# Expert steps of 512 columns a block, four places for split weights, and a written-out order of three engines, in a two-layer decoder trunk

## The chip, the cores and the metric

The kernel runs on one core of one Trainium2 chip. The metric is device time of the whole program in microseconds (us); one program computes both layers of the trunk. The engines are named PE (TensorE, matmuls), DVE (VectorE), ACT (ScalarE), POOL (GpSimd) and SP (SyncE, which only issues the loads of weights). Each engine works through its own queue in order.

## The reference

A residual stream `x` of 256 tokens by 1024 channels goes through two layers. Each layer has four token mixers and an output projection, a layer norm, a feed-forward part, a gated embedding `ple`, and a second layer norm. The feed-forward part of the second layer is a mixture of eight experts, of which each token uses two:

```python
D_MODEL, SEQ, D_FF_EXPERT, N_EXPERTS, TOP_K, MOE_BLOCK = 1024, 256, 3584, 8, 2, 128

def moe_swiglu(x, w_router, w_gate, w_up, w_down):
    logits = (xf @ w_router).astype(jnp.float32)
    top_val, top_idx = lax.top_k(logits, TOP_K)
    top_w = jax.nn.softmax(top_val, axis=-1)
    ...                      # the rows of each expert are brought together, 128 to a block
    def expert_block(args):
        xe, e = args
        return (jax.nn.silu(xe @ w_gate[e]) * (xe @ w_up[e])) @ w_down[e]
    ...                      # each row times its weight, added back to its token

        x = layer_norm(ALPHA * x + mixed, ln1_g[i], ln1_b[i])
        f = moe_swiglu(x, moe_router[i // 2], moe_w_gate[i // 2], moe_w_up[i // 2], moe_w_down[i // 2])
        ple = jax.nn.sigmoid(x @ ple_w_gate[i]) * (p[i] @ ple_w_proj[i])
        x = layer_norm(ALPHA * x + f + ple, ln2_g[i], ln2_b[i])
```

All data are float32. The weights of one expert are three matrices of 1024 x 3584 numbers, 44 MB.

## The kernel before

**Split products.** To keep float32 accuracy on PE, each weight block is split into a high piece (`whi`, made by ACT in L191) and a low piece (`wlo`, raw minus high, made by DVE in L193), and each product is three matmuls (`mm3`, L248 to L250): high by high, high by low (L249, the only one that reads `wlo`), low by high.

**Stream of weights.** `Stream` holds a list of blocks. SP loads a block into a raw buffer as soon as one is free (L157); eleven raw buffers take part in the expert stage. `take` hands out the pieces of a block, and before that calls `ahead`, which writes the splits of as many blocks as there are places for split pieces: three, the block in use among them. A place is free again when PE has done the block that stood there.

**Expert stage.** The gathered 128 rows of an expert (`rows`, by an indirect DMA of POOL from `x_rows`) are transposed by PE (`gat`) and split (`gh`/`gl`, `ghl`). Then follow four steps `j` of 896 hidden columns. `up` runs two products (`fg`, `fu`) into four banks `pff` of 448 columns each, in eight blocks (896 KB each, 12 matmuls each); ACT applies Silu to `fg` (L1512) and DVE multiplies by `fu` (L1513, tile `ffg`). `turn` transposes the 896 columns (`ftp`, L1522) and splits them (`hth`, `htl`, L565 and L566). `down` takes the `w_down` blocks of the step before (three or four, 1 MB, 12 matmuls of 512 columns each) and sums into two banks `pdn` for the whole expert. The order on PE is so: up of step j, then down of step j-1. An expert has 32 up-blocks and 14 down-blocks. PSUM banks come from two groups of four: `mm_bank` (`pff`, `ppg`) and `ax_bank` (`pdn`, `ftp`, `gat` and others).

**Side work.** Generators (`start_side`) hold work that is dealt out between blocks: `pump()`, called after every block, counts each down and runs it to its next `yield`. So `prepare` gathers the rows of the next expert, `collect` adds up the results at the end, and `turn` is one too.

**Hand-over.** Before the experts, DVE normalises two tiles of 128 tokens (L603, L604), PE transposes them (`xtp`), the router's product (`lp`) and the top-2 choice follow on PE, ACT and DVE (`lg`, `sel`, `gw`, `pos`), and four quarters of the gate product of the embedding (`ppg`, 48 matmuls of 256 columns each) run on PE meanwhile; their results are finished by DVE (`plt`) and POOL.

**Order.** In this part the program's order on SP is fixed by hand (`manual_schedule`); the order of PE, DVE, ACT and POOL is the scheduler's choice.

Of the kernel before, what the change touches and what calls it, by code (L numbers as in the profile page):

```python
# [20 lines left out]
P = 128  # L21
T = 256
NT = 2
# [74 lines left out]
def tile_trunk(ctx, tc, x, p, positions, w_in, s5_a_re, s5_a_im, s5_log_dt, s5_b_re, s5_b_im, s5_c_re, s5_c_im,  # L98
# [33 lines left out]
    class Stream:  # L132
# [41 lines left out]
        def double(self, slots):  # L174

            self.pair = [(q[0], m) for q, m in zip(self.pair, slots)]
# [940 lines left out]
    FE, PAIRS = 896, ((0, 3), (3, 7), (7, 10), (10, 14))  # L1117

    def plan_experts(add, units, wg, wu, wd, r_in, r_out, per=2):

        last = None
        of = lambda r: (r,) if per == 1 else ()

        def down():
            e, j = last
            for c in range(*PAIRS[j]):
                for r in range(0, 2, per):
                    add(("fd", e, c) + of(r), r_out(wd, e, 2 * c + r, per), [(ALL, ALL)])

        for e in units:  # L1130
            for j in range(4):
                for nm, w in (("fg", wg), ("fu", wu)):
                    for q in range(4):
                        for r in range(0, 2, per):
                            add((nm, e, j, q) + of(r), r_in(w, e, 2 * q + r, per, FE * j, FE), [(ALL, ALL)])
                if last:
                    down()
                last = e, j
        down()
# [5 lines left out]
    def down_rows(t, r0, c, n):  # L1145

        first = lambda c: r0 + FE * (c // 7) + c % 7
        return dr(t, first(c) * D, [[7 * D, P], [(first(c + 1) - first(c)) * D, n], [1, D]])
# [334 lines left out]
    def experts(units, before, down_end):  # L1483


        def pair(u, *key):

            if u.get("per") == 1:
                return [[t[:, 0] for t in u["take"](*key, r)] for r in range(2)]
            w = u["take"](*key)  # L1490
            return [[t[:, r] for t in w] for r in range(2)]

        def up(u, j):
            bk = {}
            hi, lo = u["x"]
            cols_ = [slice(FE // 2 * h, FE // 2 * (h + 1)) for h in range(2)]
            for w in ("fg", "fu"):
                bk[w] = [mm_bank("pff")[:, 0:FE // 2] for _ in range(2)]
                for q in range(4):
# [27 lines left out]
        def down(u, j, side_):  # L1527
# [3 lines left out]
            for c in range(*PAIRS[j]):  # L1531
                ab = pair(u, "fd", c)
# [418 lines left out]
```

## Time and profile before

| | |
|---|---|
| median of three runs | 1881.46 us (1880.41 to 1882.23) |
| profiled execution | 1881.37 us, span 1879.6 us |
| mean granted clock of PE in it | 0.986 of full speed |
| PE busy | 1807.0 us (96%) |
| DVE, ACT, POOL busy | 1451.9 us (77%), 1136.7 us (60%), 290.7 us (15%) |
| moved by DMA | 506.16 MB, mean 269 GB/s |
| expert stage | 860.16 to 1858.95 us of the span |

The shares are means over the whole program, in which the mixers of both layers, the dense feed-forward part of the first layer and the experts have different limits. The expert stage is more than half of the time; after it stand some 20 us for the last combination, layer norm and the store.

### The profile page before, as it was taken

The page shows a single profiled execution, that of the slowest core. Times are in us where ns is not written, and L with a number is a line of the kernel's source. Part 1 is how long each engine was busy: PE and PEld are TensorE (multiplying, and loading weights), DVE is VectorE, ACT ScalarE, POOL GpSimd, SP SyncE. Part 2 cuts the span into 40 slices and gives each one's busy share as a digit, 9 for nine tenths or more (in the row PEclk, how much of TensorE's full clock was granted, in tenths as well). Part 3 has the DMA queues.
Part 4 walks back from the last instruction along what each step waited for, and adds up shares of the span by engine and source line. Part 5 has one row for each costly group of instructions (what it writes and reads, how often), then busy time and mean ns, then how long its engine had stood idle before and what let it go on. Part 6 is the DMA issues. An engine that isn't in the chain of part 4 may idle for free. (4 is left out here: it accounts for less than half of the span.)

```text
span 1879.6 us, 26683 instructions
## 1 busy us (share of the span) xinstructions
PE 1807.0 (96%) x10669; PEld 1627.9 (87%) x10669; DVE 1451.9 (77%) x1392; ACT 1136.7 (60%) x1143; POOL 290.7 (15%) x286
## 2 busy tenths in 40 slices
PE   8999999999999999997999999999999999999995
PEld 7889989999978989986888888888888888888884
DVE  7966687554476865777888888888888988888886
ACT  5544454444435454455777777677777777777772
POOL 2755238000031210231100000000000000000011
PEclk9999999999999999998999999999999999999998
DMA  7443466555534338846999999899999999999981
GB/s 247 144 123 113 163 235 202 188 192 181 183 131 138 136 110 316 277 166 227 379 349 383 371 361 375 324 368 381 357 366 335 368 366 366 359 381 356 366 341 47
DMA packets 166681, 506.16 MB, mean 269 GB/s; under 512 B 15852, under 2 KB 30740, under 8 KB 154260
## 3 DMA queue, kind: packets, MB, share of 16 engines
q1 hardware_dynamic: 163460, 493.36, 71.7%
q0 software_dynamic: 2080, 7.35, 1.0%
q10 hardware_dynamic: 1008, 3.67, 0.5%
q8 instruction: 85, 1.39, 0.3%
q14 instruction: 48, 0.39, 0.1%
HBM read 497.52 MB, written 6.82 MB: 268 GB/s over the span
## 5 line engine op out<-in xcount | busy, mean ns | idle before, releaser
L193 DVE TENSOR_TENSOR wlo<-raw,whi 128x1792 fp32r<-128x1792 f32 (+1 forms) x368 | 769.8, 2104 | 122.1 <-ACT whi L191 92.3
L191 ACT ACTIVATE whi<-raw 128x1792 fp32r<-128x1792 f32 (+1 forms) x368 | 649.6, 1770 | 229.2 <-PE pff L250 118.6
L193 DVE TENSOR_TENSOR wparts<-raw,wparts 128x1024 fp32r<-128x1024 f32 (+1 forms) x235 | 306.0, 1308 | 188.8 <-ACT wparts L191 187.8
L191 ACT ACTIVATE wparts<-raw 128x1024 fp32r<-128x1024 f32 (+1 forms) x244 | 254.9, 1050 | 256.8 <-PE pff L250 79.3
L249 PE MATMUL pff<-wlo,ghl 128*128 128x448 f32 x896 | 328.0, 366 | 3.4 <-DVE wlo L193 3.3
L250 PE MATMUL pff<-whi,ghl 128*128 128x448 f32 x896 | 328.1, 366 | 0.0
L248 PE MATMUL pff<-whi,ghl 128*128 128x448 f32 x896 | 292.3, 369 | 0.8 <-ACT whi L191 0.8
L249 PE MATMUL pdn<-wlo,hth 128*128 128x512 f32 x448 | 179.0, 399 | 11.5 <-DVE wlo L193 11.3
L249 PEld LDWEIGHTS pff<-wlo,ghl 128*128 128x128 f32 x896 | 168.4, 188 | 20.8 <-DVE wlo L193 4.9
L250 PEld LDWEIGHTS pff<-whi,ghl 128*128 128x128 f32 x896 | 168.8, 188 | 15.5
L248 PEld LDWEIGHTS pff<-whi,ghl 128*128 128x128 f32 x896 | 166.6, 188 | 15.1 <-ACT whi L191 1.3
L250 PE MATMUL pdn<-whi,htl 128*128 128x512 f32 x448 | 178.4, 398 | 0.0
L248 PE MATMUL pdn<-whi,hth 128*128 128x512 f32 x448 | 159.9, 397 | 0.5 <-ACT whi L191 0.5
L250 PE MATMUL pgt<-xh,wparts 128*128 128x256 f32 x512 | 146.8, 287 | 1.7 <-DVE wparts L193 1.7
L249 PE MATMUL pgt<-xl,wparts 128*128 128x256 f32 x512 | 146.7, 287 | 0.0
L248 PE MATMUL pgt<-xh,wparts 128*128 128x256 f32 x512 | 146.6, 287 | 0.0
L249 PE MATMUL pff<-xl,wparts 128*128 128x256 f32 x448 | 126.5, 282 | 0.0
L248 PE MATMUL pff<-xh,wparts 128*128 128x256 f32 x448 | 126.4, 282 | 0.0
L250 PE MATMUL pff<-xh,wparts 128*128 128x256 f32 x448 | 126.4, 282 | 0.0
L249 PEld LDWEIGHTS pdn<-wlo,hth 128*128 128x128 f32 x448 | 84.9, 190 | 33.2 <-DVE wlo L193 15.3
L250 PEld LDWEIGHTS pgt<-xh,wparts 128*128 128x128 f32 x512 | 98.9, 193 | 2.6 <-DVE wparts L193 1.9
L250 PEld LDWEIGHTS pdn<-whi,htl 128*128 128x128 f32 x448 | 85.1, 190 | 18.2
(570 smaller groups left out, 3161.3 us busy)
## 6 DMA issues: line engine op xcount, KB each, us to landing
raw<-in_moe_w_gate_dram SPq DMA_DIRECT2D x128, 896.0 KB, 6.9
raw<-in_moe_w_up_dram SPq DMA_DIRECT2D x128, 896.0 KB, 7.5
raw<-in_moe_w_down_dram SPq DMA_DIRECT2D x112, 1024.0 KB, 7.2
raw<-in_w_in_dram SPq DMA_DIRECT2D x49, 1024.0 KB, 5.1
raw<-in_ff_w_gate_dram SPq DMA_DIRECT2D x14, 1024.0 KB, 5.0
raw<-in_ff_w_up_dram SPq DMA_DIRECT2D x14, 1024.0 KB, 5.0
raw<-in_ff_w_down_dram SPq DMA_DIRECT2D x14, 1024.0 KB, 4.9
raw<-in_w_branch_dram SPq DMA_DIRECT2D x8, 1024.0 KB, 5.0
```

The costliest lines, as they stand in the source:

```text
L191: S.activation(hi, src, AF.Copy)
L193: eng.tensor_tensor(lo, src, hi.bitcast(F32), op=OP.subtract)
L248: PE.matmul(o, ah, bh, start=start, stop=False)
L249: PE.matmul(o, ah, bl, start=False, stop=False)
L250: PE.matmul(o, al, bh, start=False, stop=stop)
```

## The change

- The steps of an expert are 1024, 1024, 1024 and 512 columns (`STEPS`), in up to two banks of 512 columns for each of the two products. A block of `w_gate` or `w_up` is 1 MB: 256 rows x 1024 columns, or 512 rows x 512 columns in the last step. An expert has 28 up-blocks and 14 down-blocks of 12 matmuls of 512 columns each.
- A partition gets four rows of `w_down` of a 512-row group instead of seven of an 896-row group.
- There are four places for split pieces; raw buffers go from eleven to nine.
- PE, DVE and ACT follow the order of the program from the first step of the routing to the end of the experts.
- Work is dealt out in smaller parts: `turn` does one multiply, one group of four transposes, or one split at a time; Silu comes after the first `fu` block; `gat` comes in two groups of four, each split one block later; the scaled store of an expert's result (`store`) and the last combination (`final`) are dealt out too. `prep` of the next expert starts one step earlier and waits six blocks for its rows.

```diff
         def double(self, slots):
-            self.pair = [(q[0], m) for q, m in zip(self.pair, slots)]
+            self.pair = [(q[0], m) for q, m in zip(self.pair + [(slots[0], None)], slots)]
...
-    FE, PAIRS = 896, ((0, 3), (3, 7), (7, 10), (10, 14))
+    STEPS = (2, 2, 2, 1)
...
         def up(u, j):
...
+            n = STEPS[j]
+            k = 4 // n
+
+            g = [ph["pool"].tile([P, 4, P], F32, tag="ffg", bufs=3, name="ffg") for _ in range(n)]
+            turned = lambda b: b.rearrange("t (p c) -> t c p", c=4)
             for w in ("fg", "fu"):
-                bk[w] = [mm_bank("pff")[:, 0:FE // 2] for _ in range(2)]
-                for q in range(4):
-                    ab = pair(u, w, j, q)
-                    for h in range(2):
-                        for r in range(2):
-                            kk = 2 * q + r
-                            mm3(bk[w][h], hi[:, kk, :], lo[:, kk, :], *(t[:, cols_[h]] for t in ab[r]),
+                bk[w] = [mm_bank("pff") for _ in range(n)]
+                for q in range(KD // k):
+                    ab = block(u, k, w, j, q)
+                    for h in range(n):
+                        for r in range(k):
+                            kk = k * q + r
+                            mm3(bk[w][h], hi[:, kk, :], lo[:, kk, :], *(t[:, 512 * h:512 * h + 512] for t in ab[r]),
                                 kk == 0, kk == KD - 1)
+                    if (w, q) == ("fu", 0):
+                        for h in range(n):
+                            S.activation(g[h], turned(bk["fg"][h]), AF.Silu)
                     pump()
-            g = tmp("ffg", [P, FE])
-            for h in range(2):
-                gs = g.rearrange("t (c p) -> t c p", c=7)[:, :, P // 2 * h:P // 2 * (h + 1)]
-                fg, fu = (bk[w][h].rearrange("t (p c) -> t c p", c=7) for w in ("fg", "fu"))
-                S.activation(gs, fg, AF.Silu)
-                V.tensor_tensor(gs, gs, fu, op=OP.mult)
             def turn():
-                yield 1
-                h2 = [ph["pool"].tile([P, 7, P], F32R, tag="ht" + t, bufs=2, name="ht" + t) for t in "hl"]
-                u.setdefault("h", {})[j] = h2
-                for a, n in ((0, 4), (4, 3)):
+                for h in range(n):
+                    V.tensor_tensor(g[h], g[h], turned(bk["fu"][h]), op=OP.mult)
+                    yield 1
+                for h in range(n):
                     tp = ax_bank("ftp")
-                    for c in range(n):
-                        PE.transpose(tp[:, c * P:(c + 1) * P], g[:, (a + c) * P:(a + c + 1) * P], ident)
-                    split_out(*(t[:, a:a + n, :].rearrange("p c t -> p (c t)") for t in h2), tp[:, 0:n * P])
+                    for c in range(4):
+                        PE.transpose(tp[:, c * P:(c + 1) * P], g[h][:, c, :], ident)
+                    yield 1
+                    h2 = [ph["pool"].tile([P, 4, P], F32R, tag="ht" + t, bufs=2, name="ht" + t) for t in "hl"]
+                    u.setdefault("h", {})[2 * j + h] = h2
+                    split_out(*(t.rearrange("p c t -> p (c t)") for t in h2), tp)
...
-            yield 3 if e.get("first") else 5
+            yield 3 if e.get("first") else 6
...
                     PE.transpose(b[:, k * P:(k + 1) * P], xg[:, ks], ident)
+                yield 1
                 split_out(*(t[:, 4 * k4:4 * k4 + 4, :].rearrange("p k t -> p (k t)") for t in (gh, gl)), b)
                 yield 1
...
         state = {"p": start_side(first_rows())}
+        order = tc.manual_schedule(engines={mybir.EngineType.PE, mybir.EngineType.DVE, mybir.EngineType.Activation})
+        order.__enter__()
         step_side(state["p"])
...
-        ws.double([more] * HL_BUFS)
+        ws.double([more] * (HL_BUFS + 1))
...
-            if j == 2 and e + 1 < NE:
+            if j == 1 and e + 1 < NE:
                 state["p"] = start_side(prep(e + 1))
...
         experts(es, before, down_end)
+        order.__exit__(None, None, None)
```

The order on the engines moves at three places. The first is PE's queue at the hand-over: `pp` and `ohp` are small products of the routing, `gat` the transposes of the gathered rows, `pff` the first expert product. Before:

```order
L249 MATMUL ppg<-wparts,xh 128x256
L250 MATMUL ppg<-wparts,xl 128x256
L1636 MATMUL pp<-sel,cst 128x16
L1637 MATMUL pp<-sel,ones 128x16
L1658 MATMUL ohp<-wt,oh 128x2 x2
L1682 MATMUL gat<-cst,rows 128x128 x8
L248 MATMUL pff<-whi,gh 128x448
L249 MATMUL pff<-wlo,gh 128x448
L248 MATMUL pff<-whi,gh 128x448
```

Afterwards the end of the same stretch reads:

```order
L249 MATMUL ppg<-wparts,xh 128x256
L250 MATMUL ppg<-wparts,xl 128x256
L1687 MATMUL gat<-cst,rows 128x128 x4
L248 MATMUL pff<-whi,gh 128x512
L249 MATMUL pff<-wlo,gh 128x512
L250 MATMUL pff<-whi,gl 128x512
```

All quarters `ppg` stood ahead of `pp`; now 24 `ppg` stand between `lq` and `pp`, 24 between `pp` and `ohp`, 96 between `ohp` and a first group of four `gat`, and 24 between this and the second group, shown here.

The second place is DVE's queue around the end of a step in the middle of the stage; `wlo` are the low pieces of coming blocks, `ffg` the multiply by `fu`, `htl` the low piece of the transposed columns. Before:

```order
L193 TENSOR_TENSOR wlo<-raw,whi 128x2048
L193 TENSOR_TENSOR wlo<-raw,whi 128x1792 x8
L1513 TENSOR_TENSOR ffg<-ffg,pff 128x7x64 x2
L193 TENSOR_TENSOR wlo<-raw,whi 128x2048 x2
L566 TENSOR_TENSOR htl<-ftp,hth 128x512
L566 TENSOR_TENSOR htl<-ftp,hth 128x384
L193 TENSOR_TENSOR wlo<-raw,whi 128x2048
```

Afterwards:

```order
L193 TENSOR_TENSOR wlo<-raw,whi 128x2048 x8
L1517 TENSOR_TENSOR ffg<-ffg,pff 128x512
L193 TENSOR_TENSOR wlo<-raw,whi 128x2048
L1517 TENSOR_TENSOR ffg<-ffg,pff 128x512
L193 TENSOR_TENSOR wlo<-raw,whi 128x2048 x2
L566 TENSOR_TENSOR htl<-ftp,hth 128x512
L193 TENSOR_TENSOR wlo<-raw,whi 128x2048
L566 TENSOR_TENSOR htl<-ftp,hth 128x512
```

The two multiplies stood side by side, and now have one `wlo` between them; the `htl` have moved one block back and also have a `wlo` between them.

The third place is the first `down` of an expert, while the rows of the next are turned. DVE's queue there, before:

```order
L193 TENSOR_TENSOR wlo<-raw,whi 128x2048 x2
L1513 TENSOR_TENSOR ffg<-ffg,pff 128x7x64
L566 TENSOR_TENSOR ghl<-gat,ghl 128x512 x2
L1513 TENSOR_TENSOR ffg<-ffg,pff 128x7x64
L193 TENSOR_TENSOR wlo<-raw,whi 128x2048 x2
L566 TENSOR_TENSOR htl<-ftp,hth 128x512
L566 TENSOR_TENSOR htl<-ftp,hth 128x384
```

Afterwards:

```order
L1517 TENSOR_TENSOR ffg<-ffg,pff 128x512
L193 TENSOR_TENSOR wlo<-raw,whi 128x2048
L566 TENSOR_TENSOR ghl<-gat,ghl 128x512
L1517 TENSOR_TENSOR ffg<-ffg,pff 128x512
L193 TENSOR_TENSOR wlo<-raw,whi 128x2048 x2
L566 TENSOR_TENSOR ghl<-gat,ghl 128x512
L566 TENSOR_TENSOR htl<-ftp,hth 128x512
L193 TENSOR_TENSOR wlo<-raw,whi 128x2048
L566 TENSOR_TENSOR htl<-ftp,hth 128x512
```

The two `ghl`, which stood together, are now apart, and the second of them stands behind two `wlo`. PE's queue at the same place afterwards, from the end of the third `down` block:

```order
L250 MATMUL pdn<-whi,htl 128x512
L1687 MATMUL gat<-cst,rows 128x128 x4
L1522 MATMUL ftp<-cst,ffg 128x128 x4
L248 MATMUL pdn<-whi,hth 128x512
L249 MATMUL pdn<-wlo,hth 128x512
L250 MATMUL pdn<-whi,htl 128x512
```

Twelve `pdn` further on stand the second four `ftp`, and right behind them the first `pff` of the next step. Before, `gat` came eight at once inside an `up` step.

## Rows read from the trace of the kernel before

**Rows 1.** windows (busy us (instructions) by engine, PEclk, DMA share, GB/s)

```profile
861.00:1131.00 270.00, 270.00 (x1316) 239.98 (x1316) 232.39 (x148) 200.19 (x149) 10.03 (x13) 1.00 0.95 359
1131.00:1859.00 728.00, 710.63 (x3412) 622.80 (x3411) 615.35 (x388) 518.36 (x383) 25.64 (x21) 1.00 0.92 349
```

**Rows 2.** waits of PE from 860 to 1859 (us in total, times, longest)

```profile
PE pdn L249 <- DVE wlo L193: 11.3, 7, 2.5
PE pff L249 <- DVE wlo L193: 3.3, 3, 2.2
```

**Rows 3.** timeline of PE (start us, us, instruction), three places

```profile
1140.97 0.36 PE L250 MATMUL pff<-whi,ghl 128*128 128x448 f32 x1
...
1144.65 0.61 PE L248 MATMUL pdn<-whi,hth 128*128 128x512 f32 x2
1145.52 0.98 PE L1522 MATMUL ftp<-cst,ffg 128*128 128x128 f32 x7 [0.26 <-DVE ffg L1513]
...
1854.79 0.40 PE L250 MATMUL pdn<-whi,htl 128*128 128x512 f32 x1
...
1858.95 3.59 PE L1766 MATMUL cmb<-yef,ohT 128*128 128x512 f32 x8
```

**Rows 4.** timeline of PE after one wait (idle us and releaser in brackets)

```profile
1178.82 0.50 PE L249 MATMUL pdn<-wlo,hth 128*128 128x512 f32 x1 [2.46 <-DVE wlo L193]
...
1180.45 0.63 PE L249 MATMUL pdn<-wlo,hth 128*128 128x512 f32 x1
...
1181.30 0.63 PE L248 MATMUL pdn<-whi,hth 128*128 128x512 f32 x1
```

**Rows 5.** timeline of VectorE around the same wait

```profile
1174.92 0.62 DVE L1513 TENSOR_TENSOR ffg<-ffg,pff 128x448 f32<-128x448 f32 x1 [2.01 <-PE pff L250]
1175.95 0.62 DVE L1513 TENSOR_TENSOR ffg<-ffg,pff 128x448 f32<-128x448 f32 x1 [0.40 <-PE pff L250]
1176.48 6.87 DVE L193 TENSOR_TENSOR wlo<-raw,whi 128x2048 fp32r<-128x2048 f32 x3
```

**Rows 6.** groups from 861 to 1859 (busy us, mean ns | idle before, releasers)

```profile
L193 DVE TENSOR_TENSOR wlo<-raw,whi 128x2048 fp32r<-128x2048 f32 x112 | 254.8, 2288 | 22.5 <-ACT whi L191 17.7 <-DMA raw<-in_moe_w_up_dram 1.8 <-PE pff L249 1.4
L191 ACT ACTIVATE whi<-raw 128x2048 fp32r<-128x2048 f32 x112 | 214.8, 1919 | 78.6 <-PE pff L250 54.6 <-PE pdn L250 20.7 <-DMA raw<-in_moe_w_up_dram 3.3
...
L566 DVE TENSOR_TENSOR ghl<-gat,ghl 128x512 fp32r<-128x512 f32 x14 | 9.0, 682 | 0.1
```

**Rows 7.** waits of SyncE's queue from 861 to 1859

```profile
SPq L157 <- DVE wlo L193: 349.3, 141, 5.6
SPq L157 <- PE pff L250: 334.2, 153, 12.2
```

**Rows 8.** timeline of PE, hand-over to the experts

```profile
832.84 0.28 PE L250 MATMUL lp<-xh,wrl 128*8 128x256 f32 x1
...
844.52 0.28 PE L248 MATMUL ppg<-wparts,xh 128*128 128x256 f32 x1
...
845.47 0.28 PE L250 MATMUL ppg<-wparts,xl 128*128 128x256 f32 x1
...
858.36 1.97 PE L1682 MATMUL gat<-cst,rows 128*128 128x128 f32 x8 [8.49 <-DMA rows<-x_rows,idx]
860.16 0.74 PE L248 MATMUL pff<-whi,gh 128*128 128x448 f32 x1
...
862.19 0.38 PE L248 MATMUL pff<-whi,gh 128*128 128x448 f32 x1
```

**Rows 9.** timeline of POOL, first gather

```profile
852.67 1.07 POOL L1689 DMA_INDIRECT rows<-x_rows,idx  x1 [0.17 <-DVE plt L1418]
```

**Rows 10.** timeline of VectorE, end of the normalisation

```profile
817.31 1.18 DVE L193 TENSOR_TENSOR wparts<-raw,wparts 128x1024 fp32r<-128x1024 f32 x1
...
823.56 2.35 DVE L193 TENSOR_TENSOR wparts<-raw,wparts 128x1024 fp32r<-128x1024 f32 x2
```

**Rows 11.** the page, part 2: GB/s in 40 slices of 47 us

```profile
GB/s 247 144 123 113 163 235 202 188 192 181 183 131 138 136 110 316 277 166 227 379 349 383 371 361 375 324 368 381 357 366 335 368 366 366 359 381 356 366 341 47
```

More of the change, by code (lines that the diff above doesn't have):

```diff
@@ L1145, in down_rows @@
     def down_rows(t, r0, c, n):
-        first = lambda c: r0 + FE * (c // 7) + c % 7
-        return dr(t, first(c) * D, [[7 * D, P], [(first(c + 1) - first(c)) * D, n], [1, D]])
+        return dr(t, (r0 + 512 * (c // 4) + c % 4) * D, [[4 * D, P], [D, n], [1, D]])
     def plan(i):
@@ L1483, in experts, with block @@
     def experts(units, before, down_end):
[L1486 to L1491, printed above, removed]
+        def block(u, n, *key):
+            per = u.get("per", 1)
+            parts = [u["take"](*key, *((r,) if per > 1 else ())) for r in range(per)]
+            return [[t[:, r] for t in w] for w in parts for r in range(n // per)]
         def up(u, j):
@@ L1530, in down @@
                 u["acc"] = [[ax_bank("pdn") for _ in range(2)]]
-            for c in range(*PAIRS[j]):
-                ab = pair(u, "fd", c)
+            for c in range(4 * j, 4 * j + 2 * STEPS[j]):
+                ab = block(u, 2, "fd", c)
                 for h in range(2):
@@ L1536, in down @@
                         kk = 2 * c + r
-                        lh, ll = (t[:, kk % 7, :] for t in u["h"][kk // 7])
+                        lh, ll = (t[:, kk % 4, :] for t in u["h"][kk // 4])
                         mm3(u["acc"][0][h], lh, ll, *(t[:, hs] for t in ab[r]), kk == 0, kk == 27)
                     if c == 13 and u.get("final"):
-                        u["final"](h)
+                        u["scale"](h)
                 pump()
-            if j == 3 and not u.get("final"):
-                down_end(u)
+            if j == 3:
+                (u.get("final") or down_end)(u)
         pending = None
@@ L1712, in down_end, with store @@
         def down_end(e):
-            y = ph["more"][0].tile([P, D], F32, tag="ye", bufs=2, name="ye")
-            for h in range(2):
-                S.activation(y[:, 512 * h:512 * h + 512], e["acc"][0][h], AF.Copy, scale=e["ws"])
-            nc.scalar.dma_start(y_rows[e["n"] * P:(e["n"] + 1) * P, :], y)
+            def store():
+                y = ph["more"][0].tile([P, D], F32, tag="ye", bufs=2, name="ye")
+                for h in range(2):
+                    S.activation(y[:, 512 * h:512 * h + 512], e["acc"][0][h], AF.Copy, scale=e["ws"])
+                    yield 1
+                nc.scalar.dma_start(y_rows[e["n"] * P:(e["n"] + 1) * P, :], y)
+            start_side(store())
         def numbers():
@@ L1752, in first_rows, with scale, final @@
             yield from route()
-            yield 1
             yield from prep(0)
         st = [sm.tile([P, 2, 6], F32, tag="st", name="st") for _ in range(NT)]
-        def final(h):
-            e, hs = es[-1], slice(512 * h, 512 * h + 512)
-            drain_side(state["c"], "rows of the others")
-            y = tmp("yef")
-            S.activation(y, e["acc"][0][h], AF.Copy, scale=e["ws"])
-            for tt in range(NT):
-                cb = ax_bank("cmb")
-                PE.matmul(cb, e["ohT"][:, tt * P:tt * P + P].bitcast(F32), y, start=True, stop=True)
-                V.tensor_add(pr[:, tt, hs], pr[:, tt, hs], cb)
-                V.bn_stats(st[tt][:, h, :], pr[:, tt, hs])
+        ye = []
+        def scale(h):
+            ye.append(tmp("yef"))
+            S.activation(ye[h], es[-1]["acc"][0][h], AF.Copy, scale=es[-1]["ws"])
+        def final(e):
+            drain_side(state["c"], "rows of the others")
+            for h in range(2):
+                hs = slice(512 * h, 512 * h + 512)
+                for tt in range(NT):
+                    cb = ax_bank("cmb")
+                    PE.matmul(cb, e["ohT"][:, tt * P:tt * P + P].bitcast(F32), ye[h], start=True, stop=True)
+                    V.tensor_add(pr[:, tt, hs], pr[:, tt, hs], cb)
+                    V.bn_stats(st[tt][:, h, :], pr[:, tt, hs])
         es = [dict(n=e, first=e == 0, odd=e % 2, turned=e == NE - 1, place=e % 2, take=lambda w, *k, e=e, **kw: ws.take(w, e, *k, **kw)) for e in range(NE)]
@@ L1887, in end @@
                     ph["more"] = more_pool, "more", MORE_BUFS
-                    ph["left"] = MORE_BUFS - 3
+                    ph["left"] = MORE_BUFS - 5
                     ph["gb1"] = gain_rows(ln1_g, ln1_b, i, None)
@@ L1900, in tile_trunk @@
         pool = tc.tile_pool(name="ffn%d" % i, bufs=1, reuse_waits="tile")
-        ph.update(pool=pool.__enter__(), t2=4 - last, t4=3, y=0, spare=False)
+        ph.update(pool=pool.__enter__(), t2=4, t4=3, y=0, spare=False)
         ph["tmp"] = ph["pool"]
```

40 lines of the change are left out of this document (22 added, 18 removed).

## The prediction

> **What bounds the kernel now.** Only the expert stage and the hand-over into it are touched, so I read those. First the busy times by stretch: from 861 to 1131 us PE is busy in all 270 us, and from 1131 to 1859 in 710.6 of 728 [rows 1]. So PE is the bound, perfectly fed in the first quarter and not in the rest. Then the list of PE's waits in the stage: nearly all of them stand at the second product of a step's first blocks, for the low piece `wlo` that VectorE makes (11.3 and 3.3 us) [rows 2]. Waits for DMA are not in that list.
>
> The waits miss one part. I therefore count PE's work in starts of matmuls. From 1140.97 to 1144.65 lie 18 steps of 448 columns, 3.68 us or 0.2044 us each; from 1854.79 to 1858.95 lie 18 of 512 columns, 4.16 us or 0.2311 each [rows 3]. The stage has 8 x 32 x 12 = 3072 of the first and 8 x 14 x 12 = 1344 of the second: 627.9 + 310.6 = 938.5 us. With 224 transposes `ftp` and 56 `gat` (seven take 0.98 us to the end of the last [rows 3], so 0.11 to 0.12 from start to start; 31 us) and 2.5 us for small router products (estimate), 972 us. The stage runs from 861 to the last `pdn` at 1858.95 [rows 3], 998 us. So **26 us** are lost: 17 as idle time [rows 1], the rest as matmuls at half rate just after a stall (1180.45 to 1181.30 are two steps of 0.43 us instead of 0.23, behind a wait of 2.46 us) [rows 4].
>
> Why VectorE is late is in its own rows: it stands idle 2.01 us at the multiply `ffg` (L1513), which waits for the last `pff` of the step, stands a second time at the second multiply, and only then makes three low pieces in a row, 6.87 us [rows 5]. PE meanwhile has two blocks in store (three places for split pieces, one of them in use), 2 x 12 x 0.2311 = 5.5 us, runs dry and waits until 1178.82 [rows 4]. A queue stands still, though the engine is not overloaded: a low piece takes 2.29 us of a block's 2.78 [rows 6].
>
> Transfers are not it: SyncE's loads wait for room, 349.3 us for `wlo` and 334.2 us for `pff` to release a buffer [rows 7], and ScalarE waited for the data of an 8 KB block only 3.3 us in the stage [rows 6].
>
> **The change, part by part.**
>
> *Widths.* An expert goes from 32 blocks of 448-column products and 14 of 512 to 42 of 512 (28 + 14; the bytes are the same). Before: 384 x 0.2044 + 168 x 0.2311 = 117.3 us; after: 504 x 0.2311 = 116.5. Times 8: **-6.5 us**. This is PE issue time on the critical engine, so it counts in full.
>
> *Four places, spread turn.* With four places the piece for block n+3 is made while PE works on block n. At the end of a step (t=0) the split that VectorE had before the multiply ends at about +1.4 us, the two multiplies follow with one split between them, and the first piece that is behind them is wanted by PE three blocks later, at 8.3 us; ScalarE 1.92 and VectorE 2.29 after a place comes free at 0 [rows 6] give 4.9 with one multiply (0.62 [rows 5]) between. Margin over 3 us, where before it was negative. I take away 25 of the 26 us: **-25 us** (bounds -17, the idle alone, and -26). Program order costs nothing by itself here since the same few instructions stand on each queue; what hides a longer wait of VectorE is that margin, and if it is gone each step loses what it loses today, about 1 us.
>
> *A new wait, seen in the order.* In the program order of `down` of an expert's first step (7 times), PE does 12 `pdn`, 4 `gat`, 24 `pdn`, 4 `gat`, 4 `ftp`, 12 `pdn`, 4 `ftp`. Two of the four PSUM banks for such work are held by `pdn`, so the second `ftp` needs the bank of the second `gat`, which is free only when VectorE has made its `ghl`. That stands in VectorE's queue behind two `wlo`. The second of these goes into the place that the third `pdn` block leaves. Counted from that block's end: 0.2 release, 1.92 (whi), 0.15, 2.29 (wlo), 0.68 (ghl) [rows 6], 5.2 us; PE reaches the `ftp` after 4 + 4 transposes and 12 `pdn`, 0.44 + 0.44 + 2.78 = 3.66. It stands 1.5 us, 7 times: **+10.5 us** (bounds 0, if banks fall another way, and 3 us each with half-rate matmuls after it, 21). Queued behind `ftp` is the next step's `pff`, so all of PE waits. For the other in-order waits that I can't price (the `store` of `y` on ScalarE, the later `cmb`), **+2 us** (0 to 6).
>
> *The hand-over.* Before, the last `lp` starts at 832.84, PE stands 8.49 us at `gat` for the gathered rows, and the first `pff` starts at 860.16 at half rate (0.74 us; full rate from 862.19) [rows 8], so the stage begins as if at 861.1. The gather itself was issued at 852.67 [rows 9]. In the new order three pieces `wparts` (1.18, and two in 2.35 us) [rows 10] stand behind the normalisation of the second tile, so `xl`, `lp` come 3.5 us earlier: last `lp` at about 829. From there PE has 192 `ppg` at 0.119 us (8 in 0.95 from 844.52 to 845.47 [rows 8]), 22.8 us, 8 `gat`, 0.9, and waits that I put at 2.5 (three `wparts` still ahead of `lg`, and PE cold after its idle stretch). First `pff` near 855.5. The gather leaves 96 `ppg` (11.4 us) plus 24 ahead of `gat`: against at most 5.7 us from issue to use before (852.67 to 858.36), so it is hidden; without that cover the 8.5 us come back. **-5.5 us** (bounds -9, had no wait remained, and 0).
>
> *Nothing:* `w_down` four rows to a partition instead of seven (a block still takes 8 KB of each; loads wait for room, not for data); nine raw buffers for eleven (2 fewer blocks of store, 5 us of a wait for room that the rows show to be there nearly always; without it ScalarE would wait for data); the `cmb` at the end (8 of them stood after the last `pdn` already).
>
> Sum against the profiled run's 1881.37 (the median is 1881.46): -6.5 - 25 + 10.5 + 2 - 5.5 = -24.5, **1857 us**.
>
> **A rule against it.** The stretch without stalls moved 359 GB/s [rows 1] with transfers waiting for room; slices of 47 us reach 383 [rows 11]. The forecast needs the stage's 350 MB (351 GB/s x 998 us) in 998 - 6.5 - 25 + 10.5 + 2 = 979 us, 358 GB/s, as the mean of the whole stage. The Trainium skill, "DMA: Bandwidth & Descriptors", section "Where 436 GB/s comes from", says that between HBM and SBUF the memory's share of one core, about 358 GB/s, is what binds. By it the stage could not fall under 350 MB / 358 GB/s, 978 us, nor the time under 1881 - 20 - 5.5 = 1856: the forecast would just pass and the first rival below could not come. The trace does not bear it out as a hard limit: four of those slices stand at 379 GB/s or more.
>
> **The rivals.**
> - *The new wait does not come* (a bank or queue falls better than I read): 1857 - 10.5 = 1846. For it: the order is read by hand. Against: the bank's reader does stand behind a split that only starts when PE has left its place. Chance 0.18.
> - *Transfers become the bound.* For: their share was 0.95 in the stall-free stretch [rows 1], and two buffers are gone. Against: the waits for room and the slices above 379. With 359 GB/s as the most that lasts, the stage can shrink to 975 us and the forecast stands; with the mean of 351 nothing is won in the stage and only the hand-over is left, 1876. In the middle, at 354, the stage takes 989 and the time is 1881 - 9 - 5.5 = 1867. Chance 0.12.
> - *More of the same kind of waits*: ScalarE and VectorE, now in program order, stand at an instruction whose input PE makes late at other steps too, an estimate of 0.45 us at each of 32 steps: 1857 + 14 = 1871. Chance 0.13.
> - *Slower: PE stands at the row gather.* PE's place for `gat` is now fixed, six blocks (16.7 us) after `idx` is asked for; the scheduler used to put it where the rows had come. The chain needs 2.7 us for `idx` behind a split and the gather: 5.7 at the hand-over, 11.4 were it twice that under the load of the stage. That leaves 2.6 us. Only if landing takes over 18 us does each of 7 gathers cost over 4 us, 28 us in all, and eat the gain; at 19 us it is 1857 + 35 = 1892. For: the stage's transfer queues are full. Against: ScalarE and PE waited for no gather inside the stage before. Chance 0.06.
> - *Nothing measurable* (the gains meet new waits of equal size by accident): 1878 to 1885. Chance 0.05.
>
> **How the numbers follow.** The forecast has 0.46, own range 1849 to 1865 (its bounds: old stalls -17, new wait 0 to 21, hand-over 0 to -9, not all together). Range 1843 to 1874: it takes in 1846, 1867 and 1871, and leaves out the last two rivals and the far end of the transfers' case, 0.17. A measurement of this kernel tells about 0.2%, 3.8 us, from no change: faster than 1877.7 is the forecast and the first three rivals less a tail (0.86), the same 0.06, slower 0.08 (the gather, and a part of the unknown waits).
>
> **What the profile after would show.** The waits of PE for `wlo` under 4 us in the stage; a row of PE at `ftp` waiting for VectorE's `ghl` (L566), 7 times, 1 to 2 us: if it is missing, 1846; if it is 3 us, 1868. Matmul steps of 0.231 us in `pff`. The first `pff` at 854 to 858, with `gat` not waiting for a gather. GB/s near 360 in the stage, ScalarE's waits for data still a few us: if they are tens, transfers have become the bound. PE waiting at `gat` for `rows` inside the stage would be the slower rival. I am wrong if PE's waits move to other lines with more than 20 us in sum.

## The result, and the profile after

The changed kernel takes **1855.76 us** (median of four runs, 1854.15 to 1861.62), 25.8 us less than the kernel before beside it (1881.58). The ratio is 0.9869, with a 95% interval of 0.9847 to 0.9891. The forecast was 1857, in a range from 1843 to 1874. The profiled execution took 1855.93 us with a span of 1854.1.

From the page of the changed kernel (span, busy time by engine):

```profile
span 1854.1 us, 25642 instructions
...
PE 1798.2 (97%) x10285; PEld 1550.8 (84%) x10285; DVE 1443.1 (78%) x1344; ACT 1125.3 (61%) x1095; POOL 275.6 (15%) x286
```

Its windows over the expert stage, with the columns of [rows 1]:

```profile
855.00:1125.00 270.00, 267.42 (x1196) 216.88 (x1195) 235.82 (x155) 198.08 (x134) 5.88 (x11) 1.00 0.97 366
1125.00:1835.00 710.00, 703.66 (x3148) 570.30 (x3147) 609.13 (x356) 510.41 (x350) 14.29 (x21) 1.00 0.94 357
```

PE's waits from 855 to 1835 us:

```profile
PE ftp L1522 <- DVE ghl L566: 8.9, 7, 1.4
PE pff L250 <- DVE gl L566: 0.7, 1, 0.7
```

Both rows of [rows 2], 14.6 us of waiting for `wlo`, are gone. In their place stands the one wait that the forecast had named, PE at `ftp` for VectorE's `ghl`: seven times, 8.9 us.

That wait in PE's timeline (start, duration, in brackets idle time and what ended it):

```profile
908.82 0.60 PE L1687 MATMUL gat<-cst,rows 128*128 128x128 f32 x4
909.25 0.60 PE L1522 MATMUL ftp<-cst,ffg 128*128 128x128 f32 x4
...
913.91 0.66 PE L1522 MATMUL ftp<-cst,ffg 128*128 128x128 f32 x4 [1.29 <-DVE ghl L566]
```

VectorE's timeline at the same place:

```profile
908.38 2.29 DVE L193 TENSOR_TENSOR wlo<-raw,whi 128x2048 fp32r<-128x2048 f32 x1
910.96 2.29 DVE L193 TENSOR_TENSOR wlo<-raw,whi 128x2048 fp32r<-128x2048 f32 x1 [0.29 <-ACT whi L191]
913.17 0.68 DVE L566 TENSOR_TENSOR ghl<-gat,ghl 128x512 fp32r<-128x512 f32 x1
```

The third `down` block ends at 908.82, where four `gat` begin. VectorE makes one `wlo`, stands 0.29 us, makes the next one from 910.96, and only then `ghl`, until 913.85. PE's second `ftp`, which needs the bank that `ghl` reads, starts at 913.91 after 1.29 us of standing. From the block's end to the end of `ghl` are 5.0 us; the forecast had 5.2.

The hand-over in PE's timeline (compare [rows 8]):

```profile
820.53 1.08 PE L580 MATMUL xtp<-cst,xt 128*128 128x128 f32 x4 [4.08 <-issue]
...
827.25 0.28 PE L250 MATMUL lp<-xh,wrl 128*8 128x256 f32 x1
...
834.31 0.37 PE L1640 MATMUL pp<-sel,cst 128*128 128x16 f32 x2 [0.74 <-DVE sel L1631]
...
849.54 0.60 PE L1687 MATMUL gat<-cst,rows 128*128 128x128 f32 x4
...
853.20 0.48 PE L248 MATMUL pff<-whi,gh 128*128 128x512 f32 x1
...
854.60 0.50 PE L250 MATMUL pff<-whi,gl 128*128 128x512 f32 x1 [0.70 <-DVE gl L566]
854.94 0.40 PE L248 MATMUL pff<-whi,gh 128*128 128x512 f32 x1
...
857.96 0.39 PE L249 MATMUL pff<-wlo,gh 128*128 128x512 f32 x1
```

The gather of the first rows in POOL's timeline (compare [rows 9]):

```profile
841.18 1.05 POOL L1695 DMA_INDIRECT rows<-x_rows,idx  x1 [0.17 <-issue]
```

The gather is issued at 841.18 instead of 852.67, `gat` starts at 849.54 without a wait, where it stood 8.49 us, and the first `pff` starts at 853.20 instead of 860.16. The last two PE rows also give the new spacing: 13 matmuls of 512 columns in 3.02 us, 0.2323 each.

Read off the starts of PE's rows, the 25.5 us by which the span is shorter fall into three parts. The first `pff` starts 7.0 us earlier. From it to the last `pdn` are 981.4 us (853.20 to 1834.64) instead of 998.6 (860.16 to 1858.73), 17.1 less. What follows is 1.4 us shorter.

### The profile page after: what moved, and what is told of

Its sections match the earlier page's. It is cut to its first block, busy times and chain, and to the rows that moved or that the text cites. A ratio compares the mean times of both kernels' runs of the same rounds, so it can differ in the third digit from the quotient of the medians.

```text
span 1854.1 us, 25642 instructions
## 1 busy us (share of the span) xinstructions
PE 1798.2 (97%) x10285; PEld 1550.8 (84%) x10285; DVE 1443.1 (78%) x1344; ACT 1125.3 (61%) x1095; POOL 275.6 (15%) x286
## 4 chain that ended last, share of the span: by engine, by line
PE 77%; DVE 5%; ACT 2%; issue 1%; POOL 0%; POOLq 0%; DVEq 0%; ACTq 0%
PE pff L248 14%; PE pff L250 14%; PE pff L249 14%; PE pdn L250 7%; PE pdn L248 7%; PE pdn L249 6%; PE pgt L250 2%; PE pgt L248 2%; PE pgt L249 1%; PE ftp L1522 1%; DVE wlo L193 1%; ACT whi L191 1%; DVE wparts L193 1%; DVE xt L603 1%; PE ppg L248 1%
## 5 line engine op out<-in xcount | busy, mean ns | idle before, releaser
L193 DVE TENSOR_TENSOR wlo<-raw,whi 128x2048 fp32r<-128x2048 f32 x336 | 768.5, 2292 | 129.3 <-ACT whi L191 120.4
L191 ACT ACTIVATE whi<-raw 128x2048 fp32r<-128x2048 f32 x336 | 643.4, 1918 | 244.5 <-PE pff L250 140.3
L248 PE MATMUL pff<-whi,ghl 128*128 128x512 f32 x784 | 312.8, 399 | 0.0
L250 PE MATMUL pff<-whi,ghl 128*128 128x512 f32 x784 | 309.1, 394 | 0.0
L249 PE MATMUL pff<-wlo,ghl 128*128 128x512 f32 x784 | 308.7, 394 | 0.0
L248 PE MATMUL pdn<-whi,hth 128*128 128x512 f32 x448 | 178.8, 399 | 0.0
L250 PEld LDWEIGHTS pff<-whi,ghl 128*128 128x128 f32 x784 | 147.2, 188 | 36.0
L249 PEld LDWEIGHTS pff<-wlo,ghl 128*128 128x128 f32 x784 | 147.3, 188 | 33.7
L248 PEld LDWEIGHTS pff<-whi,ghl 128*128 128x128 f32 x784 | 147.2, 188 | 33.5
```

The source lines that it names most:

```text
L191: S.activation(hi, src, AF.Copy)
L193: eng.tensor_tensor(lo, src, hi.bitcast(F32), op=OP.subtract)
L248: PE.matmul(o, ah, bh, start=start, stop=False)
L249: PE.matmul(o, ah, bl, start=False, stop=False)
L250: PE.matmul(o, al, bh, start=False, stop=stop)
```

## Experiments

Each run was timed in five rounds (5 to 12 executions) beside the kernel before, which took 1878 to 1891 us in these sessions, with medians of 1880.6 to 1883.6; times of different sessions are compared by their ratios to it. The table has for each kernel the time, the ratio with its interval, and from PE's timeline in its one profiled execution the hand-over (start of the last `ppp` to start of the first expert `pff`) and the stage (first `pff` to last `pdn`).

| kernel | us | ratio to before (95%) | hand-over | stage |
|---|---|---|---|---|
| before | 1881.6 | 1 | 43.5 | 998.6 |
| changed | 1855.8 | 0.9869 (0.9847 to 0.9891) | 37.1 | 981.4 |
| e1 changed, three places | 1866.4 | 0.9911 (0.9885 to 0.9936) | 40.4 | 982.6 |
| e2 changed, scheduler's order | 1881.4 | 0.9991 (0.9976 to 1.0007) | 51.7 | 993.3 |
| e3 scheduler's order, three places | 1872.6 | 0.9934 (0.9910 to 0.9957) | 49.7 | 983.2 |
| e4 split of the rows at once | 1845.3 | 0.9799 (0.9776 to 0.9822) | 36.8 | 971.2 |
| e5 hand-over left to the scheduler | 1864.4 | 0.9902 (0.9879 to 0.9925) | 45.5 | 981.8 |
| e7 before, in program order | 1861.9 | 0.9884 (0.9864 to 0.9904) | 40.8 | 984.0 |
| e8 e4, seven raw buffers | 1847.0 | 0.9816 (0.9792 to 0.9839) | 36.6 | 971.2 |
| e9 e4, three places | 1854.7 | 0.9833 (0.9812 to 0.9853) | 41.0 | 974.2 |
| e10 e9, old turn | 1972.6 | 1.0467 (1.0445 to 1.0490) | 40.5 | 1091.8 |
| e12 e10, four buffers | 1866.7 | 0.9913 (0.9892 to 0.9935) | 41.9 | 987.2 |
| e13 e4, rows two blocks after idx | 1882.8 | 1.0010 (0.9997 to 1.0023) | 36.9 | 1010.3 |
| e14 e4, half a quarter first | 1845.6 | 0.9810 (0.9786 to 0.9834) | 37.4 | 970.7 |

### The new wait: e4

```diff
                     PE.transpose(b[:, k * P:(k + 1) * P], xg[:, ks], ident)
-                yield 1
                 split_out(*(t[:, 4 * k4:4 * k4 + 4, :].rearrange("p k t -> p (k t)") for t in (gh, gl)), b)
```

Expected:

> The changed kernel with the split of the gathered rows right after their transposes (one wait of a block taken out in prepare), so that the bank is read ahead of the next wlo. If the wait of PE at ftp is the bank held for ghl: that row (8.9 us in 7 waits) is gone and the time is 1844 to 1848 us. Rival: the split now pushes whi and wlo of the coming block back by 0.6 and 0.7 us and the wait moves to wlo: 1852 to 1856 us.

Measured: 1845.32 us, 10.4 below the changed kernel. Of PE's waits in the stage one is left:

```profile
PE pff L250 <- DVE gl L566: 0.7, 1, 0.7
```

In the window of the stage (columns as in [rows 1]) PE is busy in all 968 us:

```profile
856.00:1824.00 968.00, 968.00 (x4333) 785.99 (x4332) 844.17 (x508) 706.87 (x484) 23.00 (x32) 1.00 0.96 364
```

The wait for the bank is shown as the cause: with `ghl` ahead of the next `wlo` it goes, and nothing takes its place. The stage is 10.3 us shorter. This is the best kernel of the study, 2.0% under the one before.

### Order or places: e1, e2, e3, e9, e7

e1 and e9 take the fourth place away (e9 with the edit of e4):

```diff
-        ws.double([more] * (HL_BUFS + 1))
+        ws.double([more] * HL_BUFS)
```

e2 and e3 take the program order away, e3 also the fourth place:

```diff
-        order = tc.manual_schedule(engines={mybir.EngineType.PE, mybir.EngineType.DVE, mybir.EngineType.Activation})
-        order.__enter__()
         step_side(state["p"])
...
         experts(es, before, down_end)
-        order.__exit__(None, None, None)
```

e7 adds these lines of order to the kernel before, and nothing else.

Expected of e1:

> The changed kernel with three places for split pieces instead of four; all else as changed. Theory A, the order did it (a split is written ahead of the multiply that waits, and one between the two multiplies): after a step's end at 0, the third down-block's piece is ready at about 4.6 us and wanted at 5.55, so hardly a wait comes back: 1856 to 1862 us, PE's waits for wlo under 5 us in the stage. Theory B, the fourth place did it: the waits for wlo come back, 8 to 25 us: 1864 to 1880 us.

Expected of e2:

> The changed kernel with the order of PE, VectorE and ScalarE left to the scheduler; four places stay. Theory A (order): waits for wlo come back in part, and the hand-over's 7 us with them: 1866 to 1880 us. Theory B (places): only the hand-over comes back and part of the wait for the bank goes: 1853 to 1864 us, PE's waits for wlo under 5 us.

Expected of e3:

> The changed kernel with the scheduler's order and three places: neither of the two remedies, only the new widths and the side work in smaller parts. Both theories: the waits for wlo are back, 15 to 30 us, and the hand-over too: 1868 to 1884 us. If it stays under 1862, the smaller parts of the side work (Silu early, the multiply and the transposes in turns) did it, and neither order nor places.

Expected of e9:

> The kernel of e4 (split of the gathered rows at once) with three places instead of four. Theory A (in this order the fourth place has next to no use in the stage): 1845 to 1851 us, waits for wlo under 4 us. Rival (the fourth place hid waits, and in e1 the wait for the bank gave VectorE time to catch up): waits for wlo of 8 us or more, 1853 to 1862.

Expected of e7:

> The kernel before with nothing changed but the program order of PE, VectorE and ScalarE over the same stretch: 896-column steps, three places, old turn. Theory A (order): a low piece now stands ahead of the multiplies, the third down-block's piece is 0 to 0.5 us late at a step's end instead of 2.5 in the bad places: waits for wlo fall from 15 to under 10 us, and 7 us come from the hand-over: 1855 to 1866. Rival (the old form of the work itself, multiplies side by side with three places): the waits for wlo stay at 15 or grow at each of 32 steps: 1872 to 1890.

PE's waits from the hand-over to the end of the experts in e1:

```profile
PE ftp L1522 <- DVE ghl L566: 9.0, 7, 1.3
PE pff L249 <- DVE wlo L193: 1.8, 1, 1.8
PE ppg L249 <- DVE wparts L193: 1.8, 1, 1.8
...
```

The same list of e7:

```profile
PE pff L249 <- DVE wlo L193: 2.7, 3, 2.0
...
```

Of e2:

```profile
PE gat L1687 <- DMA rows<-x_rows,idx: 11.9, 1, 11.9
PE pff L249 <- DVE wlo L193: 10.4, 19, 1.8
...
PE pdn L249 <- DVE wlo L193: 1.3, 1, 1.3
```

And of e3:

```profile
PE gat L1687 <- DMA rows<-x_rows,idx: 11.9, 1, 11.9
PE pff L249 <- DVE wlo L193: 4.6, 4, 1.6
PE pdn L249 <- DVE wlo L193: 2.0, 2, 1.1
...
```

In program order the waits for `wlo` are small with three places (1.8 us in e1), and small in the old kernel too, with its old steps, its old turn and three places: 2.7 us in e7, where [rows 2] have 14.6. In the scheduler's order with four places and the new turn (e2) they are 11.7. So the order is enough to remove them, as theory A says, and the fourth place is not; e3 below shows that the order is not the only way. A row of ScalarE in the kernel before, at the stall of [rows 5], shows what the order changes:

```profile
1171.04 1.92 ACT L191 ACTIVATE whi<-raw 128x2048 fp32r<-128x2048 f32 x1 [0.75 <-PE pff L250]
```

This high piece was done at 1172.96, and yet VectorE stood from 1172.91 to 1174.92 at the multiply and made the low piece afterwards. In program order the `wlo` stands ahead of the multiplies, as VectorE's timeline of e7 shows at the end of a step:

```profile
1176.87 2.29 DVE L193 TENSOR_TENSOR wlo<-raw,whi 128x2048 fp32r<-128x2048 f32 x1 [0.48 <-ACT whi L191]
...
1179.67 1.14 DVE L1513 TENSOR_TENSOR ffg<-ffg,pff 128x448 f32<-128x448 f32 x2
```

By the order alone e7 has a stage of 984.0 us instead of 998.6, and gains 2.7 us at the hand-over.

e3 was the surprise in the stage: with neither remedy its waits for `wlo` are 6.6 us, where 15 to 30 had been expected, and its stage is 983.2, nearly that of the changed kernel, which still holds the wait for the bank. The smaller parts and equal blocks do by themselves most of what the order does, in this order of the scheduler's choice; against e4 (971.2) the order is still worth some 12 us of stage. With four places (e2) the scheduler chose another order, and PE waited for `wlo` 19 times at `pff`; at 1881.4 e2 ended above what both theories allowed. Why the fourth place made it choose worse was not tried. Both lose at the hand-over what they have: PE stands 11.9 us at `gat`.

e1 and e9 took more than theory A allowed (1856 to 1862 and 1845 to 1851), though its reason held, waits for `wlo` of 1.8 and 2.1 us in the stage. Of the 9.4 us between the profiled executions of e9 and e4, 4.3 lie in the hand-over, where a `ppg` waits 1.8 us for its `wparts` as in e1, 3.0 in the stage, and the rest in the end, where the last store landed later. By the ratios the fourth place is worth some 6 to 7 us (0.9833 against 0.9799, with intervals that overlap), and by the profiles more of it lies in the hand-over than in the stage.

### The hand-over: e5, e14

e5 lets the program order begin after the embedding quarters:

```diff
-        order = tc.manual_schedule(engines={mybir.EngineType.PE, mybir.EngineType.DVE, mybir.EngineType.Activation})
-        order.__enter__()
         step_side(state["p"])
...
+        order = tc.manual_schedule(engines={mybir.EngineType.PE, mybir.EngineType.DVE, mybir.EngineType.Activation})
+        order.__enter__()
         experts(es, before, down_end)
```

Expected:

> The changed kernel with the program order beginning only at the first expert; routing and embedding quarters stay with the scheduler. Theory A (the hand-over's gain is the order there): the first pff comes 7 us later or more, with PE waiting at gat for the gathered rows: 1862 to 1872 us, and the stage from the first pff on as long as in the changed kernel (978 us from the thirteenth pff). Rival (the gain came from the smaller parts and yields of the routing): first pff within 2 us of the changed kernel, 1856 to 1859.

PE's waits of e5 at the hand-over:

```profile
PE gat L1687 <- DMA rows<-x_rows,idx: 8.2, 1, 8.2
```

Measured: 1864.39. The stage stays at 981.8, the hand-over takes 8.4 us longer, and the wait at `gat` is back with 8.2 us where it had 8.49 [rows 8]. So the gain there is the order's: the gather is asked for earlier, and `ppg` products stand between it and `gat`.

e14 puts 24 `ppg` ahead of the router's product, to fill the 4.08 us in which PE stands before the second tile's `xtp` (row 820.53 above):

```diff
+            if between is not None and tt == 0:
+                between()
+            else:
+                pump()
...
-        step_side(state["p"])
-        ple_quarter(i, 0, xh, xl, pj, pr)
+        ple_quarter(i, 0, xh, xl, pj, pr, between)
```

(`between` begins the program order and runs the first part of the routing.)

Expected:

> The kernel of e4 with the first half of the first embedding quarter (24 ppg, tokens of the first tile) written before the router's product and before the program order begins, so that it can fill PE's 4 us idle time ahead of the second tile's transposes. Theory A (PE's time at the hand-over is work plus idle time): 2.5 us of idle time filled, and 1 to 2 us of half rate after it gone: 1840 to 1843 us. Rival (the chain of the routing sets the start): the choice of experts comes later by as much, 1844 to 1847.

Measured: 1845.59, no gain over e4's 1845.32. The timeline of PE in e14 shows why:

```profile
818.72 0.39 PE L250 MATMUL ppg<-wparts,xl 128*128 128x256 f32 x1 [1.84 <-DVE xl L566]
...
821.17 0.58 PE L249 MATMUL ppg<-wparts,xh 128*128 128x256 f32 x1 [0.70 <-POOL wparts L193]
...
823.68 1.06 PE L580 MATMUL xtp<-cst,xt 128*128 128x128 f32 x4
825.05 1.12 PE L580 MATMUL xtp<-cst,xt 128*128 128x128 f32 x4 [0.31 <-DVE xt L604]
```

The products that should fill the gap wait themselves, 1.84 us for `xl` and 0.70 for `wparts`, and the first of them after a wait take 0.58 us where [rows 8] have 0.28, so that `xtp` starts at 823.68, 3.15 us later than in the changed kernel. The idle time was moved, not filled; the rival was right.

### The form of the turn: e10, e12

e10 is e9 with Silu and both multiplies at the step's end and the turn in one go:

```diff
+            for h in range(n):
+                S.activation(g[h], turned(bk["fg"][h]), AF.Silu)
+                V.tensor_tensor(g[h], g[h], turned(bk["fu"][h]), op=OP.mult)
             def turn():
-                for h in range(n):
-                    V.tensor_tensor(g[h], g[h], turned(bk["fu"][h]), op=OP.mult)
-                    yield 1
+                yield 1
                 for h in range(n):
...
-                    yield 1
```

Expected:

> The kernel of e9 (program order, three places, split at once) with the old form of turn: Silu and both multiplies right at the step's end, transposes and split in one go. Theory A (the spread of the side work is what took the waits away): the third down-block's piece is ready about 5.7 us after the step's end and wanted at 5.55, so each of 28 wide steps loses 0.2 to 0.7 us: 6 to 20 us more than e9. Rival (the equal blocks of 2.78 us did it, whatever the turn): within 3 us of e9.

Measured: 1972.59, 118 us more than e9; neither theory has that, and the question asked (do the multiplies matter) was not answered by it. Among ScalarE's waits in the stage stands:

```profile
ACT hth L565 <- PE pdn L249: 96.0, 16, 7.1
```

ScalarE's timeline at one of them:

```profile
1092.20 1.92 ACT L191 ACTIVATE whi<-raw 128x2048 fp32r<-128x2048 f32 x1 [0.86 <-PE pdn L250]
1095.41 0.60 ACT L565 ACTIVATE hth<-ftp 128x512 fp32r<-128x512 f32 x1 [1.28 <-PE ftp L1521]
1101.16 0.60 ACT L565 ACTIVATE hth<-ftp 128x512 fp32r<-128x512 f32 x1 [5.16 <-PE pdn L249]
1101.66 5.50 ACT L191 ACTIVATE whi<-raw 128x2048 fp32r<-128x2048 f32 x3
```

ScalarE stands 5.16 us at the second `hth`, until a `pdn` has read the buffer that it needs: there are two, of half a step each now. Behind it in ScalarE's queue wait three `whi` for the next step, and PE waits for the split pieces:

```profile
PE pff L248 <- ACT whi L191: 36.3, 17, 2.3
PE pff L249 <- DVE wlo L193: 27.9, 18, 2.1
...
```

In the stage of e10 PE stands 78 us, 75 more than in e9; most of the rest of the 118 is matmuls at the lower of the two clock levels: the mean granted clock over the stage was 0.95, where e9 had 1.00. So the run measured a wait for a buffer and not the multiplies. e12 gives these tiles four buffers (and leaves the raw buffers at nine):

```diff
-                    h2 = [ph["pool"].tile([P, 4, P], F32R, tag="ht" + t, bufs=2, name="ht" + t) for t in "hl"]
+                    h2 = [ph["pool"].tile([P, 4, P], F32R, tag="hu" + t, bufs=4, name="ht" + t) for t in "hl"]
```

Expected:

> The kernel of e10 with four buffers instead of two for each of the turned, split columns (hth, htl), the raw buffers still nine. Theory A: the 118 us of e10 are ScalarE standing up to 7 us at the second hth for a buffer that the down-blocks still read, with the whi of the next step queued behind; then these waits (96 us of ScalarE) go, PE's waits for whi fall under 3 us, and what is left over e9 is the wait for the bank at ftp (12 us): 1862 to 1873 us. Rival: side-by-side multiplies themselves starve the next blocks: over 1900 us.

PE's waits in e12:

```profile
PE ftp L1521 <- DVE ghl L566: 12.3, 7, 1.8
...
PE pff L249 <- DVE wlo L193: 2.3, 2, 2.1
```

Measured: 1866.66. The 118 us are gone but for 12 (15 by the ratios), and most of those are the wait for the bank, 12.3 us, which this form of the turn brings back. The waits for `wlo` are 2.3 us, with multiplies side by side and three places. So in program order the spread of the multiplies is not needed to remove the old stalls either.

### Transfers and the place of the gather: e8, e13

```diff
-                    ph["left"] = MORE_BUFS - 5
+                    ph["left"] = MORE_BUFS - 7
```

Expected of e8:

> The kernel of e4 with seven raw buffers instead of nine. Theory A (loads run ahead by more than is used): 1844 to 1849 us, ScalarE's waits for data in the stage still a few us. Rival (transfers are near the bound, and a shorter run ahead shows it): ScalarE's waits for data of tens of us, PE waits for whi and wlo, 1852 to 1870 us.

```diff
-            yield 3 if e.get("first") else 6
+            yield 3 if e.get("first") else 2
```

Expected of e13:

> The kernel of e4 with the gathered rows of experts 1 to 7 turned two blocks after idx instead of six, 11.1 us earlier, where they land 6.9 to 8.1 us ahead of their use in e4. Theory A (a place fixed in the order is a standing wait for whatever is not there; this is the slower rival of the prediction at work): PE stands at gat 3 to 4.2 us seven times, ScalarE and VectorE behind it at the split, half-rate matmuls after it: 25 to 45 us more than e4, 1870 to 1890 us. Rival (the queues ahead take up the delay, as three blocks are split ahead): under 10 us more, 1845 to 1855.

ScalarE's group `whi` in e8 (busy us, mean ns | idle before it and what ended most of it):

```profile
L191 ACT ACTIVATE whi<-raw 128x2048 fp32r<-128x2048 f32 x333 | 633.5, 1916 | 226.4 <-PE pff L250 141.1 <-PE pdn L250 76.0 <-ACT whi L191 3.5
```

PE's wait at `gat` in e13:

```profile
PE gat L1687 <- DMA rows<-x_rows,idx: 25.0, 7, 4.2
```

The first of these in PE's timeline:

```profile
894.30 1.11 PE L1687 MATMUL gat<-cst,rows 128*128 128x128 f32 x4 [3.04 <-DMA rows<-x_rows,idx]
895.07 0.77 PE L248 MATMUL pff<-whi,gh 128*128 128x512 f32 x1
...
896.06 0.63 PE L250 MATMUL pff<-whi,gl 128*128 128x512 f32 x1
896.49 0.63 PE L248 MATMUL pff<-whi,gh 128*128 128x512 f32 x1
```

The clock in e13 behind that wait (columns as in [rows 1]; PEclk is the third number from the end):

```profile
894.00:897.40 3.40, 3.10 (x10) 2.61 (x11) 0.97 (x2) 1.95 (x2) 0.00 (x0) 0.50 1.02 419
```

With seven raw buffers no transfer appears among what ended ScalarE's idle time, and the stage has the same 971.2 us: transfers do not bind, with 364 GB/s over the stage of e4. e13 ends where the kernel before does, at 1882.8: PE stands at `gat` seven times for 25.0 us, and behind each wait come five to eleven matmuls at 0.43 us instead of 0.23 (896.06 to 896.49 is one such step), with a granted clock of 0.50, that is 1.2 of 2.4 GHz. 25 us of standing cost 39 us of stage (1010.3 against 971.2).

## Why the prediction was right, point by point

- **What bounds it.** PE's issue, with stalls for `wlo`: right. With all stalls removed (e4) PE is busy without a gap in 968 us.
- **Old stalls, -25.** The size was right: both rows are gone, and the losses counted below fall by 23.3 us from the kernel before to e4. The reason was half wrong. The step put the gain down to four places and the spread turn, and said of the program order only that it costs nothing. e7, e9 and e12 show that the order is enough with three places (2.7, 2.1 and 2.3 us of waits left; in e7 and e12 with the multiplies side by side), and e2 that places and turn without it leave 11.7. The smaller parts and equal blocks are a second way to much of it: e3, without order and fourth place, leaves 6.6.
- **The new wait, +10.5.** Right in place, count (7) and cause; 8.9 us by the wait row, 10.3 us by e4's stage. No half rate followed these waits of 1.3 us, as taken. Of the +2 for other waits none came at `store` or `cmb`; the one other wait is 0.70 us for `gl`.
- **Widths, -6.5.** Right in sign, too large: `pff` at 512 columns runs at 0.2323 us a matmul (the rows of 854.94 and 857.96), not at the 0.2311 of `pdn`. With 0.2323 the prediction's own count gives 3.5 us. If a loss is each gap between starts of PE's matmuls over 0.32 us, less 0.23, then the stage loses 25.2 us in the kernel before, 11.9 in the changed one and 1.9 in e4. The stage of e4 is 27.4 us shorter than before; less the 23.3 us of losses, about 4 us are left for the widths.
- **Hand-over, -5.5.** 7.0 by the first `pff`, 6.3 counted from the last `ppp`. The waits that I had put at 2.5 us were 0.74 at `pp` and, later, 0.70 for the first `gl`; even so the stretch from the last `lp` to the first `pff` took 26 us, as the sum had it (22.8 + 0.9 + 2.5). Most of the miss is the start of that stretch: the last `lp` came at 827.25, not at about 829. The gather is hidden, as said, by the products ahead of `gat`.
- **Nothing for raw buffers and `w_down`'s rows.** Right for the buffers (e8). The layout of `w_down` was not tried alone; ScalarE waited for no data in the stage of the changed kernel or of e8.
- **The rule of 358 GB/s.** The Trainium skill, "DMA: Bandwidth & Descriptors", section "Where 436 GB/s comes from", has the memory's share of a core bind at about 358. The trace, of one core that runs alone, does not agree: 366 GB/s for 270 us in the changed kernel and 364 over all 968 us of e4's stage, with loads still waiting for room (SyncE's queue in e4 waits 371 us for `wlo` and 285 us for `pff` to free a buffer). e4's stage of 971.2 us lies under the 978 that the prediction worked out by that rule.
- **The rivals.** The first (no new wait, 1846) did not come by itself, but e4 made it so, and its number held: 1845.3. Transfers as the bound did not come: the mean over the stage could rise to 364 GB/s in e4, and e8 lost nothing with fewer buffers. More waits of the same kind at other steps did not come either, by the two rows of waits of the changed kernel. The slower one (PE at the row gather) did not come because the rows of experts 1 to 7 land 7.0 to 8.5 us ahead of their use, not the 2.6 that I took as the bad case; e13 shows that the mechanism is real and where it decides.

The measured terms are -7.0 for the hand-over, -13.3 for the losses in the stage (25.2 to 11.9: all old stalls gone, 10.0 for the bank and 1.9 of small ones left), about -4 for the widths and -1.4 at the end, where the last store landed sooner; the span shrank by 25.5. The widths' term is what the losses leave over, so that the sum closes is no test of it. Nor is the end shown to be the change's: from the last instruction of POOL to the end of the span it was 7.4 us before, 5.7 in the changed kernel, 5.6 in e4 and 7.8 in e9. That the forecast came within 1.3 us is partly luck: it credited 2.5 us too much to the widths and some 2 too much to the old stalls, charged 2 for waits that did not come, credited 1.5 too little to the hand-over, and had nothing for the end.

## What to carry to other kernels

A fixed order is worth what it puts ahead of a waiting instruction: look for the engine that stands at an instruction while work behind it is ready, and compare how long the queue stands with how long its readers can go on. The same order makes every late thing a standing wait, so count for each instruction in it what it waits for, and how far ahead that is: a bank read behind two splits cost 10 us, a gather used four blocks too early 39, a buffer count that no longer fits 118. Before crediting a gain to the part of a change that looks strongest, undo the parts one at a time.

## What the runs showed that I had not expected

- Half rate after a wait can cost half as much again as the wait: 25.0 us of standing at `gat` lengthened e13's stage by 39.2. After the waits of 1.3 us at `ftp` it did not come; after 2.46 us in [rows 4] and after all seven waits of 3.0 to 4.2 us in e13 it did. The length of the wait alone does not tell: in the kernel before, another wait of 2.46 us, before the `pdn` at 1429.90, was followed by steps of 0.23 us at a granted clock of 1.00 (window below, columns as in [rows 1]), and the one of 1.95 us before 1838.31 by a clock of 0.50.

```profile
1429.90:1434.00 4.10, 4.10 (x18) 3.35 (x19) 4.01 (x2) 1.48 (x1) 0.00 (x0) 1.00 0.97 360
```

- A matmul of 512 columns takes 0.2323 us in `pff` and 0.2311 in `pdn`; what makes this difference was not tried.
- The granted clock differs between executions in stretches that no edit touches. Between 200 and 400 us, with PE equally busy, it was 0.97 in the profile of e3 (windows, columns as in [rows 1]):

```profile
200.00:400.00 200.00, 196.11 (x1407) 186.22 (x1407) 137.45 (x136) 95.82 (x118) 65.41 (x39) 0.97 0.59 194
```

and 1.00 in that of the changed kernel:

```profile
200.00:400.00 200.00, 196.10 (x1428) 184.89 (x1428) 139.10 (x138) 98.95 (x121) 65.95 (x39) 1.00 0.60 198
```

The experts of e3 therefore began later than the table's columns explain; so the stretches are compared there, and the totals by all rounds.
